# First mixer of a two-layer encoder: score matmuls of two heads interleaved, division moved behind the values, state reordering split over two engines, ten low weight parts written by an accumulating DMA

## The chip, the cores and the metric

The kernel runs as one program on one core of one Trainium2 chip. The metric is the device time of one execution in microseconds, the median of three runs. TensorE (PE) does the matmuls, ScalarE (ACT) and VectorE (DVE) the elementwise work, GpSimd (POOL) some more of it, and SyncE (SP) issues nearly all DMAs.

## The reference, cut to what matters

Two layers over 512 positions of width 1024. The change lies in the first mixer alone: an 8-head neighbourhood attention beside a bidirectional S5 state recurrence, both fed by one input projection.

```python
def na_s5_mixer(h, w_in, ...):
    z = h @ w_in                                   # 1024 -> 4 x 512
    q, k, v, u = jnp.split(z, 4, axis=-1)
    a_out = neighbourhood_attention(q, k, v, rpb)  # 8 heads of 64
    b_out = s5_glu(s5_bidirectional(u, ...), w_glu, b_glu)
    return jnp.concatenate([a_out, b_out], -1) @ w_out

# attention, per head and row of the 8 x 64 grid
logits = q_row . k_window * dh**-0.5 + bias        # 8 x 16 window
probs  = softmax(logits)
out    = probs @ v_window

# S5, per direction, 32 groups of 16 channels, 64 states
bu     = b_bar @ u
states = associative_scan(lam_bar, bu)
y     += real(c @ states)
```

After the mixer come, per layer, a gated MLP and a per-layer embedding p that is projected to the model width; the second layer has a retention mixer. The change touches none of them.

## The kernel before, in words

All matrix products of the projections are done in split precision: weights and activations are kept as a high part and a low part, and `mm3` (L134 to L137) issues three matmuls for each product, low weight by high activation (L135), high by high (L136) and high weight by low activation (L137), all into one PSUM bank.

The weights lie in DRAM as 241 chunks of 128x1024 (512 KB, eight 128x128 tiles each) in the order of use. For each chunk SP issues the load into a raw buffer `wr` (L98, three buffers), ACT copies the high part `wh` (L113), and DVE subtracts the low part `wl` = `wr` - `wh` (L115 for chunks 1 to 3, L117 after that). `wh` and `wl` have four buffers each, so chunk c can be split once PE has finished chunk c-4; `weights()` asks for the split three chunks ahead. Chunks 0 to 3 give U (the input of the recurrence), 4 to 11 give q and k, 12 to 15 give v, 16 to 19 the projections of p, 20 to 23 the first half of the output projection.

The first mixer, in the order of its code:

- U projection, then `u_out` (DVE, L162 inside a helper): U times the normalising row, written to DRAM and read back in another layout (SP). It needs the row `rr`, which ACT copies at L249.
- q and k, eight outputs n = 0 to 7 (DVE L679 or L162 reads each out of PSUM). Between them DVE builds the weights of the recurrence: `prep_w1` (four products, two sums), which `trans_w1` transposes on PE (L481) and ACT copies (L483); with them `states` (PE, L585) makes the inputs of the recurrence into `XV`. `prep_w2` (three DVE operations of 128x512) makes the output weights; the table `W2_K` says how many after each n.
- v, four banks at once, and among it the `local` steps of the recurrence (four DVE operations each).
- Thirteen score steps. Step h of 0 to 7 does `scores(h)`: eight matmuls for one head (L752; 64 of the 128 rows hold the head, rows 0 to 63 for an even head, 64 to 127 for an odd one), a DVE reduction with the bias (L758) and an ACT exponential (L761, which also gives the sums). `scale(h)` (DVE) takes reciprocals of the sums and multiplies the exponentials. `transp(h-3)` transposes them on PE (L778) and ACT copies the result (L780). `values(m)` for two heads (L797) multiplies with v, and ACT (high) and DVE (low) split the result straight out of PSUM. Between these lie `strips` (PE L501, ACT L504 into the table `Tm`), the carry steps of the recurrence (`carry`, four DVE operations of 128x512 each, seven in all, placed by `CARRY_A` and `CARRY_F`), and `fill(n)`: n outputs of the projection of p, six matmuls each, which are independent work for PE. When all eight strips are done, `toeplitz` sends `Tm` through DRAM and back (SP, eight loads, L526).
- `first_half(n)`, the first half of the output projection, six of them; after the fifth `phases(b)` reorders the finished states `XV` into matmul operands, on ACT (L884 for partitions 0 to 63, L886 for 64 to 127, eight each).
- `y_mm` (PE, L904, 96 matmuls in 192 records), which needs U, `Tm`, the w2 weights and the reordered states, and gives the output of the recurrence.

The code states this order, but a scheduler decides on each engine what stands next (up to the end of `u_out` the order of ACT and DVE is as written). PSUM has eight banks of 128x512, the pool of 128x512 tiles in SBUF 53.

Of the kernel before, what the change touches and what calls it, by code (L numbers as in the profile page):

```python
# [41 lines left out]
SPLIT_AHEAD = 3  # L42
GLU_AT = 10
FILL = (0,) + (1,) * 11
W2_K = (0, 0, 0, 1, 1, 2, 2, 2)
W2_A = (1, 1, 1, 1, 1, 1, 1, 1, 0, 0, 0, 0, 0)
CARRY_A = (0, 0, 0, 0, 0, 0, 0, 0, 1, 1, 1, 1, 1)
LOCAL_V = (1, 2, 2, 2)
CARRY_F = (1, 1, 0, 0, 0)
HELD = 5  # L50
LAG = 3
HOLD = 2
# [3 lines left out]
DO_W = 6  # L56
PLE_POOL = 3
NOLAG = 7


@with_exitstack
def trunk_kernel(ctx, tc, xn, xp, pT, wts, vec, s5bc, ddiag, bias, cs, dst, ident, out):
# [20 lines left out]
    def PS():  # L83
        seq[0] += 1
        return pp.tile([128, 512], F32, name=f"ps{seq[0]}", tag="ps")
# [22 lines left out]
    def w_split1(c):  # L108
        w_dma(c)
        raw = raws.pop(c)  # L110
        h = wspl.tile([128, 1024], F32R, name=f"wh{c}", tag="wh")
        l = wspl.tile([128, 1024], F32R, name=f"wl{c}", tag="wl")
        act.activation(out=h, in_=raw, func=ACTF.Copy)  # L113
        if c < 4:
            dve.tensor_tensor(out=l, in0=raw, in1=f(h), op=ALU.subtract)  # L115
        else:
            late.append(lambda: dve.tensor_tensor(out=l, in0=raw, in1=f(h), op=ALU.subtract))  # L117
            if len(late) > 1:
                late.pop(0)()
        parts[c] = (h, l)  # L120
        st["split"] += 1
        w_dma(c + RAW_BUFS)
# [38 lines left out]
    def tt(eng, out, a, b, op):  # L161
        eng.tensor_tensor(out=out, in0=a, in1=b, op=op)  # L162
# [117 lines left out]
    def mixer0():  # L280
# [455 lines left out]
        P2 = {}  # L736
        PTs = {}

        def scores(h):
            rows = slice(64 * (h % 2), 64 * (h % 2) + 64)  # L740
            q, k = qt[h // 2], kt[h // 2]
            bt = bts.pop(h)
            bias_load(h + 2)
            for half in range(2):
                ps = PS()
                for i in range(2):
                    b = 2 * half + i
                    if b < 3:
                        lhs, rhs = q[rows, 64 + 128 * b:192 + 128 * b], k[rows, 128 * b:128 * b + 256]
                    else:  # L750
                        lhs, rhs = qe[h // 2][rows], k[rows].rearrange("p (a t) -> p a t", t=128)[:, ::3, :]
                    pe.matmul(out=ps[:, 256 * i:256 * i + 256], lhsT=lhs, rhs=rhs, start=True, stop=True)  # L752
                P = T()
                for i in range(2):
                    b = 2 * half + i
                    v = 256 * (b == 3)

                    dve.tensor_tensor_reduce(out=P[:, 256 * i:256 * i + 256], in0=ps[:, 256 * i:256 * i + 256],  # L758
                                             in1=bt[:, v:v + 256], scale=-1.0, scalar=3e38, op0=ALU.add,
                                             op1=ALU.min, accum_out=mx[:, h, b:b + 1])  # L760
                    act.activation(out=P[:, 256 * i:256 * i + 256], in_=P[:, 256 * i:256 * i + 256], func=ACTF.Exp,  # L761
                                   scale=-1.0, bias=mx[:, h, b:b + 1], accum_out=sums[:, h, b:b + 1])
                P2[h, half] = P

        def scale(h):
            for half in range(2):
                P = P2[h, half]
                dve.reciprocal(out=sums[:, h, 2 * half:2 * half + 2], in_=sums[:, h, 2 * half:2 * half + 2])
                sc = sums[:, h, 2 * half:2 * half + 2].rearrange("p (a o) -> p a o", o=1).to_broadcast([128, 2, 256])
                Pv = P.rearrange("p (a k) -> p a k", a=2)  # L770
                tt(dve, Pv, Pv, sc, ALU.mult)

        def transp(h):
            for half in range(2):
# [7 lines left out]

        def values(m):

            ps = PS()
# [14 lines left out]
            for e in range(2):  # L800
                for half in range(2):
                    PTs.pop((2 * m + e, half))
            h_, l_ = T(F32R), T(F32R)
            act.activation(out=h_, in_=ps, func=ACTF.Copy)
            tt(dve, l_, ps, f(h_), ALU.subtract)
            mix.append((h_, l_))

        kept = []

# [26 lines left out]

        for step in range(10 + LAG):
            if step < 8:
                scores(step)
            if LAG <= step < 8 + LAG:  # L840
                transp(step - LAG)
            next_w2(W2_A[step])
            if step == 2:
                fk_load(1)
            if step == 6:
                prep_chunk()
            if step < 8:
                scale(step)
            run("carry", CARRY_A[step])
            if step >= LAG + 2 and (step - LAG) % 2 == 0:  # L850
                values((step - LAG) // 2 - 1)
            next_strips()
            if step < len(FILL):
                fill(FILL[step])
            if step >= 9:
                x_load(2)
        fill(16)
        keep()
        fk.clear()
# [10 lines left out]
                    between(k)  # L870
            tt(dve, xr[n], ps, xr[n], ALU.add)


        sph = {}

        def phases(b):
            gs = slice(8 * b, 8 * b + 8)
            for c in range(2):
                t = T()
                v = t.rearrange("p (g c) -> p g c", c=64)  # L880
                eng = dve
                eng.memset(v[0:64, :, 0:1], 0.0)
                eng.memset(v[64:128, :, 63:64], 0.0)
                act.activation(out=v[0:64, :, 1:64], in_=XV[0:64, c, 0:63, gs].rearrange("p c g -> p g c"),  # L884
                               func=ACTF.Copy)
                act.activation(out=v[64:128, :, 0:63], in_=XV[64:128, c, 62::-1, gs].rearrange("p c g -> p g c"),  # L886
                               func=ACTF.Copy)
                sph[b, c] = v

        flat = XV.rearrange("p a b c -> p (a b c)")  # L890
        G = flat[:, 0:2048].rearrange("p (m j i n) -> p m j i n", m=2, j=8, n=16)
# [31 lines left out]
                        dve.tensor_copy(YG[:, 2 * m + e, 4 * jh:4 * jh + 4, :], src)  # L923

        for n in range(HELD):
            run("carry", CARRY_F[n])
            first_half(n)
        for b in range(4):
            phases(b)
        first_half(HELD)  # L930
        for m in range(2):
            for i in range(8):
# [438 lines left out]
```

## Time and profile before

| what | value |
|---|---|
| median of 3 runs | 1541.13 us (1540.98 to 1542.32) |
| the profiled execution | 1541.97 us, span 1540.2 us |
| PE busy | 1501.5 us, 97% of the span |
| DVE, ACT, POOL busy | 928.9, 613.6, 355.1 us |
| mean granted TensorE clock | 0.988 of full speed |

A trace row gives a start, a duration, the engine, the line of the kernel, and output and inputs by the program's names. "Idle before" is the time in which the engine stood still ahead of an instruction, with what ended it. The granted clock is that of TensorE as a share of full speed (2.4 GHz); 0.5 is its lower level (1.2 GHz).

### The profile page before, as it was taken

The page shows a single profiled execution, that of the slowest core. Times are in us where ns is not written, and L with a number is a line of the kernel's source. Part 1 is how long each engine was busy: PE and PEld are TensorE (multiplying, and loading weights), DVE is VectorE, ACT ScalarE, POOL GpSimd, SP SyncE. Part 2 cuts the span into 40 slices and gives each one's busy share as a digit, 9 for nine tenths or more (in the row PEclk, how much of TensorE's full clock was granted, in tenths as well). Part 3 has the DMA queues.
Part 4 walks back from the last instruction along what each step waited for, and adds up shares of the span by engine and source line. Part 5 has one row for each costly group of instructions (what it writes and reads, how often), then busy time and mean ns, then how long its engine had stood idle before and what let it go on. Part 6 is the DMA issues. An engine that isn't in the chain of part 4 may idle for free.

```text
span 1540.2 us, 18035 instructions
## 1 busy us (share of the span) xinstructions
PE 1501.5 (97%) x7088; PEld 1237.5 (80%) x7088; DVE 928.9 (60%) x1247; ACT 613.6 (40%) x853; POOL 355.1 (23%) x246
## 2 busy tenths in 40 slices
PE   7899989999999999999999999999999999999997
PEld 5787767888888888887888888888888888888886
DVE  8888974786776633476454454535367767643336
ACT  5244647454444422343425242423244444432233
POOL 0000000233232311054123141504223232312105
PEclk9899999999999999999999999999999999999999
DMA  5514191333333433433222222222333333333341
GB/s 194 150 56 154 62 249 44 96 96 98 98 102 98 119 97 96 129 107 106 83 69 82 69 82 69 83 69 82 96 96 96 96 97 97 98 96 92 99 133 55
DMA packets 57493, 153.69 MB, mean 100 GB/s; under 512 B 11584, under 2 KB 15808, under 8 KB 57408
## 3 DMA queue, kind: packets, MB, share of 16 engines
q1 hardware_dynamic: 57408, 152.55, 32.8%
q8 instruction: 55, 0.90, 0.3%
q14 instruction: 30, 0.25, 0.1%
HBM read 144.69 MB, written 7.83 MB: 99 GB/s over the span
## 4 chain that ended last, share of the span: by engine, by line
PE 81%; issue 7%; DVE 6%; DMA 2%; ACT 2%; POOL 1%; SPq 1%; DVEq 0%; POOLq 0%
PE ps L135 26%; PE ps L137 26%; PE ps L136 26%; DVE t L162 3%; PE ps L585 1%; DVE wl L117 1%; DMA wr<-in_wts_dram 1%; DMA Tm<-k_scr 1%; PE ps L752 1%; DVE t L271 1%; ACT t L884 0%; ACT t L886 0%; PE ps L778 0%; PE ps L235 0%; PE ps L481 0%
## 5 line engine op out<-in xcount | busy, mean ns | idle before, releaser
L135 PE MATMUL ps<-t,wl 128*128 128x512 f32 x1568 | 615.9, 393 | 9.6 <-DVE wl L545 7.0
L136 PE MATMUL ps<-t,wh 128*128 128x512 f32 x1568 | 611.5, 390 | 0.0
L137 PE MATMUL ps<-t,wh 128*128 128x512 f32 x1568 | 608.8, 390 | 0.7 <-DVE t L271 0.7
L117 DVE TENSOR_TENSOR wl<-wr,wh 128x1024 fp32r<-128x1024 f32 x238 | 310.2, 1305 | 306.6 <-ACT wh L113 306.4
L113 ACT ACTIVATE wh<-wr 128x1024 fp32r<-128x1024 f32 x241 | 254.6, 1059 | 583.9 <-PE ps L137 281.9
L135 PEld LDWEIGHTS ps<-t,wl 128*128 128x128 f32 x1568 | 296.1, 189 | 73.2 <-DVE wl L545 7.0
L137 PEld LDWEIGHTS ps<-t,wh 128*128 128x128 f32 x1568 | 296.0, 189 | 63.6 <-DVE t L271 1.8
L136 PEld LDWEIGHTS ps<-t,wh 128*128 128x128 f32 x1568 | 296.3, 189 | 60.3
L162 POOL TENSOR_TENSOR t<-t,t 128x512 f32<-128x512 f32 x117 | 178.1, 1524 | 457.7 <-ACT t L995 279.5
L162 DVE TENSOR_TENSOR t<-ps,t 128x512 f32<-128x512 f32 (+2 forms) x86 | 59.3, 699 | 108.5 <-PE ps L137 100.0
L162 DVE TENSOR_TENSOR t<-t,t 128x512 f32<-128x512 f32 (+2 forms) x113 | 96.9, 877 | 27.8 <-ACT t L194 20.7
L162 DVE TENSOR_TENSOR pad<-ps,t 128x512 f32<-128x512 f32 x88 | 60.6, 692 | 82.7 <-PE ps L137 82.7
L991 DVE SCALAR_TENSOR_TENSOR t<-pad,vecs,t 128x512 f32<-128x512 f32 x88 | 102.2, 1164 | 1.5
L162 POOL TENSOR_TENSOR t<-t 128x512 f32<-128x512 f32 x33 | 50.4, 1529 | 189.9 <-DVE t L162 189.9
L135 PE MATMUL ps<-e,wl 128*128 128x512 f32 x216 | 85.4, 395 | 0.0
L137 PE MATMUL ps<-e,wh 128*128 128x512 f32 x216 | 85.3, 395 | 0.0
L136 PE MATMUL ps<-e,wh 128*128 128x512 f32 x216 | 85.2, 395 | 0.0
L169 POOL TENSOR_TENSOR t<-t,t 128x512 fp32r<-128x512 f32 x41 | 58.5, 1444 | 60.4 <-ACT t L168 51.7
L992 DVE SCALAR_TENSOR_TENSOR t<-pad,vecs,t 128x512 f32<-128x512 f32 x88 | 70.0, 796 | 2.9
L989 ACT ACTIVATE t<-pad,vecs 128x512 f32<-128x512 f32 x88 | 70.2, 802 | 3.4 <-DVE pad L162 3.4
L162 POOL TENSOR_TENSOR r<-v,mhalf 128x4 f32<-128x4 f32 x10 | 17.8, 1777 | 206.0 <-DVE v L239 206.0
L135 PE MATMUL ps<-wh,t 128*128 128x512 f32 x160 | 62.6, 391 | 0.0
(209 smaller groups left out, 1365.2 us busy)
## 6 DMA issues: line engine op xcount, KB each, us to landing
wr<-in_wts_dram SPq DMA_DIRECT2D x241, 512.0 KB, 3.7
pj_scr<-t SPq DMA_DIRECT2D x16, 256.0 KB, 4.8
t<-pj_scr SPq DMA_DIRECT2D x16, 256.0 KB, 4.5
t<-in_xp_dram SPq DMA_DIRECT2D x8, 256.0 KB, 5.4
t<-in_bias_dram SPq DMA_DIRECT2D x8, 256.0 KB, 3.9
Tm<-k_scr SPq DMA_DIRECT2D x8, 256.0 KB, 7.6
t<-in_xn_dram SPq DMA_DIRECT2D x8, 256.0 KB, 7.3
out_dram<-t SPq DMA_DIRECT2D x8, 256.0 KB, 2.4
```

What stands on the lines that cost most here:

```text
L113: act.activation(out=h, in_=raw, func=ACTF.Copy)
L117: late.append(lambda: dve.tensor_tensor(out=l, in0=raw, in1=f(h), op=ALU.subtract))
L135: pe.matmul(out=ps, lhsT=lhs[1], rhs=rhs[0], start=start, stop=False)
L136: pe.matmul(out=ps, lhsT=lhs[0], rhs=rhs[0], start=False, stop=False)
L137: pe.matmul(out=ps, lhsT=lhs[0], rhs=rhs[1], start=False, stop=stop)
L162: eng.tensor_tensor(out=out, in0=a, in1=b, op=op)
L169: low.tensor_tensor(out=l, in0=src, in1=f(h), op=ALU.subtract)
L271: self.late.append(lambda: dve.scalar_tensor_tensor(out=l, in0=x, scalar=g, in1=f(h), op0=ALU.mult, op1=ALU.subtract))
L585: pe.matmul(out=pw[:, i, :], lhsT=w1t["ri"[c], g // 4][:, 128 * (g % 4):128 * (g % 4) + 128], rhs=U[:, g, :], start=True, stop=True)
L989: act.activation(out=c, in_=t[:, 1:513], func=ACTF.Identity, scale=vcol(cw + 44 + j), bias=vcol(V_CB + 44 * i + j))
L991: dve.scalar_tensor_tensor(out=c, in0=t[:, 0:512], scalar=vcol(cw + j), in1=c, op0=ALU.mult, op1=ALU.add)
L992: dve.scalar_tensor_tensor(out=c, in0=t[:, 2:514], scalar=vcol(cw + 88 + j), in1=c, op0=ALU.mult, op1=ALU.add)
```

## The change

1. **Low parts of chunks 6 to 15.** ACT writes `wl` = -`wr` (rounded as the high part is), and a DMA on POOL's queue adds the weights from DRAM into it. Ten DVE subtractions go; ten ACT operations of 128x1024 and ten accumulating transfers of 512 KB come.
2. **Scores.** `scores(m)` issues the sixteen matmuls of two heads together, alternately on rows 0 to 63 and 64 to 127, into four PSUM banks; the softmax part is `soft(h)`.
3. **Division.** `scale` goes (sixteen DVE products of 128x512). `values(m)` spreads the reciprocal sums over a second bank `pr` with eight matmuls (L801 of the changed kernel), ACT copies it, DVE multiplies it with the values, and the product is split. Per pair of heads that is one ACT copy and one DVE product more, and one bank.
4. **Tables.** Three `prep_w2` move from the score steps into the q and k part; all seven carries run in steps 5 to 11; `prep_chunk` (small DVE operations that the carries need) moves from step 6 to step 3.
5. **Phases.** They move ahead of `fill(16)`, each with one fill behind it, and the half for partitions 64 to 127 is copied by DVE.

```diff
-W2_K = (0, 0, 0, 1, 1, 2, 2, 2)
-W2_A = (1, 1, 1, 1, 1, 1, 1, 1, 0, 0, 0, 0, 0)
-CARRY_A = (0, 0, 0, 0, 0, 0, 0, 0, 1, 1, 1, 1, 1)
+W2_K = (0, 0, 0, 1, 1, 3, 3, 3)
+W2_A = (1, 1, 1, 1, 1, 0, 0, 0, 0, 0, 0, 0, 0)
+CARRY_A = (0, 0, 0, 0, 0, 1, 1, 1, 1, 1, 1, 1, 0)
-CARRY_F = (1, 1, 0, 0, 0)
+WL_DMA = (6, 16)
...
         act.activation(out=h, in_=raw, func=ACTF.Copy)
-        if c < 4:
+        if WL_DMA[0] <= c < WL_DMA[1]:
+            while late:
+                late.pop(0)()
+
+            act.activation(out=l, in_=raw, func=ACTF.Copy, scale=-1.0)
+            pool.dma_start(out=l, in_=wts[c], accum_op=ALU.add)
+        elif c < 4:
             dve.tensor_tensor(out=l, in0=raw, in1=f(h), op=ALU.subtract)
...
+        def scores(m):
+            for half in range(2):
+                for e in range(2):
+                    sps[2 * m + e, half] = PS()
+                for i in range(2):
+                    b = 2 * half + i
+                    for e in range(2):
+                        rows = slice(64 * e, 64 * e + 64)
...
+                        pe.matmul(out=sps[2 * m + e, half][:, 256 * i:256 * i + 256], lhsT=lhs, rhs=rhs,
+                                  start=True, stop=True)
...
-        def scale(h):
-            for half in range(2):
-                P = P2[h, half]
-                dve.reciprocal(out=sums[:, h, 2 * half:2 * half + 2], in_=sums[:, h, 2 * half:2 * half + 2])
-                sc = sums[:, h, 2 * half:2 * half + 2].rearrange("p (a o) -> p a o", o=1).to_broadcast([128, 2, 256])
-                Pv = P.rearrange("p (a k) -> p a k", a=2)
-                tt(dve, Pv, Pv, sc, ALU.mult)
...
-            ps = PS()
+            ps, pr = PS(), PS()
+            for b in range(4):
+                for e in range(2):
...
+                    pe.matmul(out=o, lhsT=sums[:, 2 * m + e, b:b + 1].to_broadcast([128, 64]), rhs=idn,
+                              start=True, stop=True)
+            rs = T()
+            act.activation(out=rs, in_=pr, func=ACTF.Copy)
...
-            h_, l_ = T(F32R), T(F32R)
-            act.activation(out=h_, in_=ps, func=ACTF.Copy)
-            tt(dve, l_, ps, f(h_), ALU.subtract)
-            mix.append((h_, l_))
+            tt(dve, rs, ps, rs, ALU.mult)
+            mix.append(split(rs))
...
             if step < 8:
-                scores(step)
+                if step % 2 == 0:
+                    scores(step // 2)
+                soft(step)
...
-            if step == 6:
+            if step == 3:
                 prep_chunk()
             if step < 8:
-                scale(step)
+                dve.reciprocal(out=sums[:, step, :], in_=sums[:, step, :])
...
-                act.activation(out=v[64:128, :, 0:63], in_=XV[64:128, c, 62::-1, gs].rearrange("p c g -> p g c"),
-                               func=ACTF.Copy)
+                dve.tensor_copy(v[64:128, :, 0:63], XV[64:128, c, 62::-1, gs].rearrange("p c g -> p g c"))
...
+        for b in range(4):
+            phases(b)
+            fill(1)
+        fill(16)
...
         for n in range(HELD):
-            run("carry", CARRY_F[n])
             first_half(n)
-        for b in range(4):
-            phases(b)
         first_half(HELD)
```

Lines behind the first hunks stand some 6 lower in the changed kernel, later ones up to 22 (L752 of before is L761, L904 is L926). Where the change moves instructions, the built order shows it at three places.

DVE from the end of U's normalisation (`r50` is the row's source; `ps38` to `ps49` are the four U banks that `u_out` reads), before:

```order
L117 TENSOR_TENSOR wl6_395<-wr6_258,wh6_394 128x1024
L117 TENSOR_TENSOR wl7_439<-wr7_326,wh7_438 128x1024
L117 TENSOR_TENSOR wl8_517<-wr8_362,wh8_516 128x1024
L162 TENSOR_TENSOR t54_475<-ps38_287,t53_473 128x512
L162 TENSOR_TENSOR t55_479<-ps43_322,t53_473 128x512
L162 TENSOR_TENSOR t56_483<-ps46_357,t53_473 128x512
L162 TENSOR_TENSOR t57_487<-ps49_393,t53_473 128x512
```

Three subtractions of 128x1024 stand ahead of the four rows of `u_out`; the same place in the changed kernel, and further on the first weights of the recurrence (`t58` and `t60` are what PE transposes first):

```order
L168 TENSOR_TENSOR t54_478<-ps38_287,t53_476 128x512
L168 TENSOR_TENSOR t55_482<-ps43_322,t53_476 128x512
L168 TENSOR_TENSOR t56_486<-ps46_357,t53_476 128x512
L168 TENSOR_TENSOR t57_490<-ps49_393,t53_476 128x512
...
L685 SCALAR_TENSOR_TENSOR t68_550<-ps67_518,t53_476 128x512
L168 TENSOR_TENSOR t58_496<-t58_496,t59_497 128x512
L168 TENSOR_TENSOR t73_566<-p1r_131,t39_312 128x512
L168 TENSOR_TENSOR t74_567<-p1i_132,t41_317 128x512
L168 TENSOR_TENSOR t75_571<-p1r_131,t41_317 128x512
L168 TENSOR_TENSOR t76_572<-p1i_132,t39_312 128x512
L168 TENSOR_TENSOR t60_501<-t60_501,t61_502 128x512
```

The subtractions are gone, wl9 (which stood just ahead of the sum t58) too, and t58, which came behind all twelve products, now comes ahead of the last four.

ACT at the same place (`t53` is the row `rr` that `u_out` waits for, L255 of the changed kernel, L249 of before), in the changed kernel:

```order
L113 ACTIVATE wh6_394<-wr6_258 128x1024
L118 ACTIVATE wl6_395<-wr6_258 128x1024
L113 ACTIVATE wh7_440<-wr7_326 128x1024
L118 ACTIVATE wl7_441<-wr7_326 128x1024
L118 ACTIVATE wl8_520<-wr8_362 128x1024
L113 ACTIVATE wh8_519<-wr8_362 128x1024
L255 ACTIVATE t53_476<-ps52_471 128x512
L118 ACTIVATE wl9_598<-wr9_400 128x1024
```

Before, only wh6, wh7 and wh8 stood ahead of the row; now an operation of 128x1024 more stands behind each raw load, and chunk 8 has two ahead of the row.

PE at the start of the score steps (`t106` is k of heads 0 and 1, `t62` their q), before:

```order
L752 MATMUL ps194_1281<-t106_764,t62_503 128x256 x2
L752 MATMUL ps196_1289<-t106_764,t62_503 128x256
L752 MATMUL ps196_1289<-t106_764,qe0_1265 128x256
L501 MATMUL ps200_1306<-t99_718,t77_576 32x128 x4
L501 MATMUL ps200_1306<-t113_802,t79_584 32x128 x4
L752 MATMUL ps202_1318<-t106_764,t62_503 128x256 x2
L752 MATMUL ps204_1326<-t106_764,t62_503 128x256
L752 MATMUL ps204_1326<-t106_764,qe0_1265 128x256
```

Each head stands in one block with strips between them. The same place in the changed kernel:

```order
L761 MATMUL ps199_1304<-t106_771,t62_506 128x256
L761 MATMUL ps200_1305<-t106_771,t62_506 128x256
L761 MATMUL ps199_1304<-t106_771,t62_506 128x256
L761 MATMUL ps200_1305<-t106_771,t62_506 128x256
L761 MATMUL ps201_1310<-t106_771,t62_506 128x256
L761 MATMUL ps202_1311<-t106_771,t62_506 128x256
L761 MATMUL ps201_1310<-t106_771,qe0_1290 128x256
L761 MATMUL ps202_1311<-t106_771,qe0_1290 128x256
```

The two heads now alternate from row to row, and the strips have moved behind them; the second pair of heads alternates only in part (two rows of one head, two of the other).

ACT at the phases, before (L823 copies a fill's bank, L113 splits a chunk):

```order
L823 ACTIVATE t356_2045<-ps355_2038 128x512
L113 ACTIVATE wh24_2096<-wr24_1892 128x1024
L113 ACTIVATE wh25_2130<-wr25_2007 128x1024
L884 ACTIVATE t366_2149<-XV_84 64x8x63
L886 ACTIVATE t366_2149<-XV_84 64x8x63
L884 ACTIVATE t367_2154<-XV_84 64x8x63
L886 ACTIVATE t367_2154<-XV_84 64x8x63
```

All sixteen stand in one block behind the last fill and behind chunk 25. The same work in the changed kernel (L887 is the half that ACT keeps, L840 copies a fill's bank):

```order
L804 ACTIVATE t350_1997<-ps349_1988 128x512
L174 ACTIVATE t351_2016<-t350_1997 128x512
L840 ACTIVATE t354_2027<-ps353_2020 128x512
L887 ACTIVATE t359_2038<-XV_84 64x8x63
L887 ACTIVATE t360_2043<-XV_84 64x8x63
L840 ACTIVATE t362_2055<-ps361_2048 128x512
L887 ACTIVATE t363_2058<-XV_84 64x8x63
L887 ACTIVATE t364_2063<-XV_84 64x8x63
L840 ACTIVATE t366_2081<-ps365_2068 128x512
L887 ACTIVATE t367_2084<-XV_84 64x8x63
L113 ACTIVATE wh23_2136<-wr23_1670 128x1024
```

The eight that ACT keeps have moved up among the last fills' copies, five of them ahead of chunk 23 and none behind chunk 24.

## Rows read from the trace of the kernel before

**Rows 1.** Head of the page: busy us, share of the span, instructions.

```profile
PE 1501.5 (97%) x7088; PEld 1237.5 (80%) x7088; DVE 928.9 (60%) x1247; ACT 613.6 (40%) x853; POOL 355.1 (23%) x246
```

**Rows 2.** Stretches: length, engines' busy us (instructions), granted clock, DMA share, GB/s.

```profile
60.00:80.00 20.00, 18.02 (x79) 16.23 (x80) 14.83 (x28) 6.13 (x13) 0.00 (x0) 0.66 0.16 53
...
140.00:160.00 20.00, 16.09 (x119) 11.20 (x118) 19.48 (x63) 15.17 (x46) 0.00 (x0) 0.89 0.43 145
...
220.00:240.00 20.00, 12.64 (x120) 10.73 (x118) 5.42 (x23) 14.81 (x15) 0.00 (x0) 0.74 0.39 153
```

**Rows 3.** PE's waits from 0 to 280 us: total, times, longest.

```profile
PE ps L481 <- DVE t L162: 5.4, 1, 5.4
...
PE ps L778 <- DVE t L162: 3.9, 2, 2.5
...
PE ps L904 <- ACT t L886: 8.8, 4, 3.2
```

**Rows 4.** The chain that ended last, 38 to 76 us: start, duration, what.

```profile
47.47 3.97 DVE t L162 x4
...
60.19 1.14 DVE wl L117
...
61.98 1.97 PE ps L481 x8
63.95 3.31 PE ps L585 x16
...
74.75 0.23 PE ps L137
```

**Rows 5.** ACT in order of time, 30 to 46 us.

```profile
31.48 2.96 ACT L113 ACTIVATE wh<-wr 128x1024 fp32r<-128x1024 f32 x3
...
44.57 1.06 ACT L113 ACTIVATE wh<-wr 128x1024 fp32r<-128x1024 f32 x1 [1.98 <-DMA wr<-in_wts_dram]
45.54 0.58 ACT L249 ACTIVATE t<-ps 128x512 f32<-128x512 f32 x1
```

**Rows 6.** Stretches of 2 us, columns as in the second group.

```profile
70.00:72.00 2.00, 2.00 (x10) 1.90 (x10) 2.00 (x4) 1.48 (x3) 0.00 (x0) 0.50 0.85 217
...
156.00:158.00 2.00, 1.23 (x8) 0.90 (x12) 2.00 (x8) 1.70 (x8) 0.00 (x0) 0.50 0.00 0
...
162.00:164.00 2.00, 2.00 (x9) 1.43 (x8) 1.75 (x6) 0.64 (x2) 0.00 (x0) 0.88 0.50 140
```

**Rows 7.** PE in order of time, at 139, 169 and 188 us.

```profile
139.55 1.56 PE L752 MATMUL ps<-t,t 64*128 64x256 f32 x6
140.95 0.59 PE L752 MATMUL ps<-t,qe 64*128 64x256 f32 x2
...
169.10 1.09 PE L778 MATMUL ps<-idn,t 128*128 128x128 f32 x8
170.12 1.97 PE L797 MATMUL ps<-t,t 128*64 128x128 f32 x32
...
188.80 0.43 PE L501 MATMUL ps<-t,t 128*32 128x128 f32 x8
```

**Rows 8.** Groups by line and shape, 139 to 171 us: busy, mean ns.

```profile
L758 DVE CUSTOM_DVE_ANT_0 t<-ps,t 128x256 f32<-128x256 f32 x24 | 9.0, 418 | 0.6 <-PE ps L752 0.5
```

**Rows 9.** The chain that ended last, 200 to 250 us.

```profile
202.69 8.98 DMA Tm<-k_scr
...
225.08 1.07 ACT t L884
...
242.32 4.58 PE ps L904 x78
```

**Rows 10.** The line L904: its matmuls with `Tm`, duration, first and last start.

```profile
L904 PE MATMUL ps<-Tm,U x64: 272/273/475, 223.0 to 246.2; 128*64 128x128 f32 x64
```

**Rows 11.** DMA issues of the page: count, KB each, us to landing.

```profile
wr<-in_wts_dram SPq DMA_DIRECT2D x241, 512.0 KB, 3.7
...
Tm<-k_scr SPq DMA_DIRECT2D x8, 256.0 KB, 7.6
```

More of the change, by code (lines that the diff above doesn't have):

```diff
@@ L737, in mixer0, with soft @@
         PTs = {}
-        def scores(h):
-            rows = slice(64 * (h % 2), 64 * (h % 2) + 64)
-            q, k = qt[h // 2], kt[h // 2]
+        sps = {}
+        def scores(m):
[6 more added lines that the diff above has]
+                        rows = slice(64 * e, 64 * e + 64)
+                        q, k = qt[m], kt[m]
+                        if b < 3:
+                            lhs, rhs = q[rows, 64 + 128 * b:192 + 128 * b], k[rows, 128 * b:128 * b + 256]
+                        else:
+                            lhs, rhs = qe[m][rows], k[rows].rearrange("p (a t) -> p a t", t=128)[:, ::3, :]
+                        pe.matmul(out=sps[2 * m + e, half][:, 256 * i:256 * i + 256], lhsT=lhs, rhs=rhs,
+                                  start=True, stop=True)
+        def soft(h):
             bt = bts.pop(h)
@@ L744, in scores @@
             for half in range(2):
-                ps = PS()
[L746 to L752, printed above, removed]
+                ps = sps.pop((h, half))
                 P = T()
@@ L783, in values @@
         def values(m):
-            ps = PS()
+            ps, pr = PS(), PS()
+            for b in range(4):
+                for e in range(2):
+                    ov = pr[64 * e:64 * e + 64, :].rearrange("p (r c) -> p c r", c=64)
+                    if b < 3:
+                        o = ov[:, 8 + 16 * b:24 + 16 * b, :]
+                    else:
+                        o = ov.rearrange("p (a e) r -> p a e r", e=8)[:, ::7]
+                    pe.matmul(out=o, lhsT=sums[:, 2 * m + e, b:b + 1].to_broadcast([128, 64]), rhs=idn,
+                              start=True, stop=True)
+            rs = T()
+            act.activation(out=rs, in_=pr, func=ACTF.Copy)
             for half in range(2):
@@ L856, in mixer0, with phases @@
                 x_load(2)
+        sph = {}
+        def phases(b):
+            gs = slice(8 * b, 8 * b + 8)
+            for c in range(2):
+                t = T()
+                v = t.rearrange("p (g c) -> p g c", c=64)
+                eng = dve
+                eng.memset(v[0:64, :, 0:1], 0.0)
+                eng.memset(v[64:128, :, 63:64], 0.0)
+                act.activation(out=v[0:64, :, 1:64], in_=XV[0:64, c, 0:63, gs].rearrange("p c g -> p g c"),
+                               func=ACTF.Copy)
+                dve.tensor_copy(v[64:128, :, 0:63], XV[64:128, c, 62::-1, gs].rearrange("p c g -> p g c"))
+                sph[b, c] = v
+        for b in range(4):
+            phases(b)
+            fill(1)
         fill(16)
@@ L871, in first_half @@
             tt(dve, xr[n], ps, xr[n], ALU.add)
[L874 to L884, printed above, removed]
-                               func=ACTF.Copy)
-                act.activation(out=v[64:128, :, 0:63], in_=XV[64:128, c, 62::-1, gs].rearrange("p c g -> p g c"),
-                               func=ACTF.Copy)
-                sph[b, c] = v
         flat = XV.rearrange("p a b c -> p (a b c)")
```

## Prediction

> **What bounds the kernel now.** I read the page's busy times first, then PE's busy time and clock by stretches, then PE's waits, then the chain of work in the stretches where PE stood still. The reader should see that PE is the limit: it is busy 1501.5 us, 97% [rows 1]. So little can be won outside PE's gaps. They lie in the first mixer, and each has a second cost behind it, the clock.
>
> - Gap A, at 57 us: PE waits 5.4 us for a DVE result that its first transposes need [rows 3]. The chain shows why: `u_out` at 47.47, behind it the products for the first weights, one more subtraction (wl9, 1.14), and only then the transposes at 61.98 and the states at 63.95 [rows 4]. The clock is still 0.50 in 70 to 72 us [rows 6], and averages 0.66 over 60 to 80 [rows 2].
> - Gap B, 140 to 162 us: PE waits 3.9 us in two pieces for DVE before it can transpose the first exponentials [rows 3]. DVE is busy 19.48 of the 20 us from 140 on [rows 2]: `scale` stands in its queue behind other work. The clock falls to 0.50 in 156 to 158 us and is still 0.88 on average in 162 to 164 [rows 6].
> - Gap C, 223 to 247 us: the first matmuls of `y_mm` start at 223.0, the last with `Tm` at 246.2 [rows 10], while ACT copies the phases one by one from 225.08, 1.07 us each [rows 9]; 8.8 us of PE's waits there name L886 outright [rows 3], and the clock averages 0.74 [rows 2].
>
> Behind 260 us the program is untouched, and I count nothing there.
>
> **The change part by part.**
>
> *A: low parts by DMA.* Ten DVE subtractions of 1.14 us go. Ahead of the states four of them stood on DVE: wl6 to wl8 before `u_out`, wl9 after it. The first three win nothing, because `u_out` also waits for the row that ACT copies at 45.54 [rows 5], and ACT now has an operation more ahead of it. Chunk 8's raw load lets ACT begin at 44.57 [rows 5]; two operations of 1.06 and the row's 0.58 end at 47.3, against a start of `u_out` at 47.47 [rows 4]. So DVE starts at the same time. Between `u_out`'s end at 51.44 and wl9 at 60.19 lie fifteen operations in 8.75 us, 0.58 each [rows 4]. The first sum now stands ahead of the last four products and without wl9, so the first transposes can start 1.14 + 4 x 0.58 = 3.5 us earlier; the second sum, for the transposes that the states need, stands behind them all and wins 1.14 plus a copy between the two sums that now comes later (0.28 to 0.58). I take 1.6 us. The low end is a loss of 2 (ACT, with twice the work per chunk, late with the row by one more operation of 1.06, and the read-back of U late by one more load on SP's queue), the high end is this and the clock: at 0.50, the work from 61.98 to 72 takes 10 us for 5 at full speed, so 1.6 + 5 = 6.6.
>
> What the ten transfers cost: ACT's ten further operations lie beside PE and ACT was idle 13.87 of 20 us in 60 to 80 [rows 2]. If that cover were gone, 10 x 1.06 = 10.6 us. Each transfer must land before its chunk is used. No accumulating transfer and none on POOL's queue stands in the trace; the nearest rows are the raw loads (512 KB in 3.7 us) and `Tm` back from DRAM (256 KB in 7.6) [rows 11]. By these I bound one transfer between 3.7 and 15.2 us (twice the second, for twice the bytes). A chunk's buffers come free three chunks ahead, 72 matmuls of 0.23 us at full clock [rows 4], 5.5 us a chunk or 16.6 in all. Within these bounds less the 2.1 us of ACT none is late as long as they don't queue up behind one another: term 0, the rest under the rivals. On POOL's queue the root that the row needs stands behind the first transfer, four clears of tiles behind the next three: an issue that holds POOL delays the row and so `u_out` by as much, which the low end of -2 covers.
>
> Of this the Trainium skill speaks in "SBUF — State Buffer", section "SBUF: two separate sides": a transfer issued from POOL's queue has its descriptors written by POOL, which is locked out while DVE runs a two-port operation, so that one of 620 ns took 3100 ns beside a DVE copy. By that rule the transfers would stretch wherever DVE runs copies; the trace has no transfer of this kind with which to agree or not. By the same skill's "DMA: Bandwidth & Descriptors", section on the anatomy of one such DMA, 512 KB would take about 2.0 + 1.2 = 3.2 us, an estimate from its fit, and the term would stay 0.
>
> *B: scores, division, tables.* The first transposes no longer wait for `scale` in a full DVE queue, and three `prep_w2` leave that queue as well. I take the 3.9 us back, and the half clock that followed: in 156 to 158 PE ran 1.23 us, in 162 to 164 a mean of 0.88 is 0.5 us at half [rows 6], with the 4 us between some 5.7 us at half speed, so 2.8 lost. Interleaved scores: one head takes 2.0 us of PE (139.55 to 140.95 + 0.59, six records and two [rows 7]), eight heads 16. If rows 0 to 63 and 64 to 127 work side by side, half of it goes, 8; if not, nothing. No row has two row halves together. The nearest pair is `values`, whose matmuls alternate between the two halves of the output columns and take 1.97/32 = 62 ns a record, against 1.09/8 = 136 ns for whole transposes of the same 128 columns [rows 7]: side by side, they run at under half. I take 6 of 8, since one pair of heads in four does not alternate throughout. What the division adds on PE: eight matmuls per pair of heads, of the same form as those of `values`, 16 records of 62 ns, 1.0 us, four times 4.0.
>
> The Trainium skill bears on the first of these: "TensorE: Matmul & The Clock Gate", "Part 3: Packing small matmuls — row/col tiling", says that matmuls on different row groups of the array run at the same time, four of them measured 3.07 times as fast. The row of column halves points the same way, and by two full halves the term would be 8, not 6.
>
> New waits: a pair of heads now holds four PSUM banks at once until DVE has reduced them, at 0.42 us each quarter [rows 8]; eight quarters are 3.4 us, and PE has two strips and one fill to do between. The next `values` wants two banks. I take 3 us for these, between 0 and 6. B is then 3.9 + 2.8 + 6 - 4.0 - 3 = 5.7 us, with ends of 3.9 + 2.8 + 0 - 4.0 - 6 = -3.3 and 3.9 + 2.8 + 8 - 4.0 = 10.7.
>
> *C: phases ahead.* `y_mm` takes 23.9 us from its first start at 223.0 [rows 10] to its end at 246.9. Its last 78 records took 4.58 us [rows 9], so all 192 need 11.3: 12.6 us to win. For that its inputs must be there when PE comes, at about 223.0 - 1.6 - 5.7 = 215.7. The last carry stands beside values(3) in DVE's new order; from there PE has three fills and six `first_half`, 18 + 72 matmuls or 20.7 us. ACT's eight phases of 1.07 [rows 9] with four bank copies between them need about 11, DVE's eight run beside them (no row for that copy; DVE's other strided copies are shorter than ACT's 1.07, and at 1.07 each it is 8.6). The margin is some 9 us. `Tm`: its last strips now stand ten fills, two `values`, six `first_half` and 24 transposes ahead of `y_mm`, some 39 us (132 x 0.23, 2 x 3.0 and 24 x 0.136); before, they stood at 188.80 [rows 7] and `Tm` landed at 202.69 + 8.98 = 211.7 [rows 9], 22.9 later. So both inputs are early and I take all 12.6; half of it if one is late.
>
> *Sum.* 1.6 + 5.7 + 12.6 = 19.9 us. The profiled execution's own time of 1541.97 (its span and 1.77 around it) less this is 1522.1; the median of the runs shown is 0.84 lower, so I predict 1521 (1521.2).
>
> **The rivals.**
>
> 1. *The transfers queue up (slower).* If POOL's queue moves them one after the other at L us each, the first starts when ACT has written wl6, at 31.48 + 2.96 + 1.06 = 35.5 [rows 5], and the tenth lands at 35.5 + 10 L. Chunk 15 is needed a chunk ahead of the first score, at 139.55 - 5.5 = 134.0 [rows 7]. Nothing is lost up to L = 9.9; at L = 11.9 the 20 us are gone; at the bound of 15.2 the tenth lands at 187.5, 53 late, and the time is 1521 + 53 = 1574. For it: a read, an addition and a write, in a queue for which there is no row. The rule of the Trainium skill's "SBUF — State Buffer" above would be a way to it. Against: 512 KB in 3.7 us, and DMA engines 16% busy in that stretch [rows 2]. 6%.
> 2. *Row halves don't overlap.* The term of 6 falls away: 1527. For it: no row shows it. Against: the column halves. 14%.
> 3. *Gap A heals with its clock.* The transposes that come 3.5 us earlier split the wait, and if the clock stays up another 5 us come: 1516. 10%.
> 4. *`y_mm` still waits.* DVE, which keeps the carries and now takes half the phases, or SP's queue is late with one input: 6 of 12.6 us, 1527. For it: DVE's load [rows 2]. Against: the margins. 9%.
> 5. *Nothing is won, the stall only moves:* the PSUM banks and DVE hold the score steps so long that B is -3.3 and phases are late as well: 1521 + 9 + 6 = 1536 or more. 4%.
>
> **How the numbers follow.** The forecast itself has 57%, with a range of its own of 1516 to 1526. The 80% range takes in rivals 2 to 4 with their own spread: 1511 to 1531. This kernel's runs spread 0.1%, and I call 0.2% (3 us) the least that can be told from no change. Slower by more than that needs rival 1 beyond L = 12.2: 5%. Within it: the rest of rivals 1 and 5, 2%. Faster: 93%.
>
> **What would show it.** In the changed kernel's trace: first states (L591) at about 62 us; no wait of L786 on DVE's products near 152; a pair of heads' scores in about 2.4 us, not 4; `y_mm` (L926) in one run of about 11 us from about 215, at clock 1.00; PE's wait on a low part of chunks 6 to 15 none; the transfers landing in under 10 us each. The prediction is wrong if L141 waits for a transfer between 50 and 139 us, if the scores take 2 us per head as before, or if L926 begins on time and then stops for L887, L889 or `Tm`.

## The result and the profile after

The changed kernel takes 1528.34 us (median of four runs, 1527.03 to 1530.21), the kernel before in the same comparison 1541.72: the ratio is 0.9913, 95% interval 0.9894 to 0.9932. That is 13.4 us won, where 20 were forecast. The profiled execution shown here took 1527.03 us.

The head of its page and two of its DMA rows (count, KB, median us to landing):

```profile
span 1525.2 us, 18170 instructions
...
PE 1495.3 (98%) x7152; PEld 1234.6 (81%) x7152; DVE 915.7 (60%) x1225; ACT 615.1 (40%) x859; POOL 363.9 (24%) x256
...
wl<-in_wts_dram POOLq DMA_DIRECT2D x10, 512.0 KB, 7.5
...
Tm<-k_scr SPq DMA_DIRECT2D x8, 256.0 KB, 6.7
```

PE is still the limit. Its busy time is 6 us lower than in [rows 1]; the rest of the gain is idle time that is gone. The same stretches as in [rows 2], with 160 to 180 us added:

```profile
60.00:80.00 20.00, 16.03 (x63) 13.88 (x64) 13.82 (x28) 6.14 (x12) 0.86 (x1) 0.58 0.68 169
140.00:160.00 20.00, 19.15 (x176) 14.23 (x174) 19.57 (x58) 15.96 (x47) 0.00 (x0) 1.00 0.58 187
160.00:180.00 20.00, 17.05 (x202) 13.41 (x198) 19.70 (x73) 15.85 (x46) 0.00 (x0) 1.00 0.23 78
220.00:240.00 20.00, 20.00 (x242) 18.18 (x241) 7.75 (x13) 9.85 (x16) 0.00 (x0) 1.00 0.15 48
```

Gap C is gone: PE is busy throughout 220 to 240 us at full clock. Gap B keeps its clock, though PE is still idle 0.85 + 2.95 us beside a DVE that is as full as before. Gap A has become worse: less PE work, a clock of 0.58 instead of 0.66, and the DMA engines 68% busy instead of 16%. PE's waits from 0 to 100 and 100 to 200 us, which answer to [rows 3]:

```profile
PE ps L487 <- DVE t L168: 6.2, 2, 4.3
...
PE ps L786 <- ACT t L804: 1.4, 1, 1.4
```

The chain that ended last from 46 to 74 us, against [rows 4] and [rows 5]:

```profile
46.01 0.59 ACT wl L118
...
46.96 1.04 ACT wh L113
48.00 0.49 ACT t L255
...
48.51 4.06 DVE t L168 x4
52.57 2.72 DVE t L331
55.29 2.40 DVE t L168 x4
...
64.95 1.12 PE ps L487 x4
...
66.20 7.06 PE ps L591 x32
```

ACT's row is there at 48.5, `u_out` starts 1.0 us later than before, and the small operation behind it (L331), which takes 0.42 us in e1 and e8 below, takes 2.72 on the chain (2.80 by its own record). POOL in order of time says what ran beside it:

```profile
52.22 0.85 POOL L119 DMA_DIRECT2D wl<-in_wts_dram  x1 [3.96 <-ACT wl L118]
52.75 2.25 POOL L443 MEMSET t<- 128x512 f32 x4
```

The four clears had moved behind wl9's transfer, and so beside L331. The states start at 66.20 instead of 63.95, 32 records at half clock, and the first score comes at 142.95 instead of 139.55 [rows 7]. The scores themselves, and the line of `y_mm` (duration, first and last start):

```profile
142.95 1.57 PE L761 MATMUL ps<-t,t 64*128 64x256 f32 x12
144.34 0.60 PE L761 MATMUL ps<-t,qe 64*128 64x256 f32 x4
144.87 1.08 PE L507 MATMUL ps<-t,t 128*32 128x128 f32 x32
```

```profile
L926 PE MATMUL ps<-Tm,U x64: 272/273/323, 220.6 to 230.5; 128*64 128x128 f32 x64
```

Two heads take 1.92 us (142.95 to 144.87), the time of one before. `y_mm` runs from 220.6 to some 231.3 (its last matmul starts at 231.0), 10.7 us, where it took 23.9.

The balance by stages of the two profiled executions: up to the first score 139.55 to 142.95, 3.4 us lost; from there to `y_mm` 83.5 to 77.7, 5.8 won; `y_mm` 23.9 to 10.7, 13.2 won. That makes 15.6 where the spans differ by 15.0. The 0.6 is lost behind `y_mm`, in the untouched rest of the program, which takes between 1293.3 and 1295.0 us in the fourteen profiled executions of this document.

### The profile page after: what moved, and what is told of

Same layout as the page of the kernel before. It is cut to its first block, busy times and chain, and to the rows that moved or that the text cites. A ratio compares the mean times of both kernels' runs of the same rounds, so it can differ in the third digit from the quotient of the medians.

```text
span 1525.2 us, 18170 instructions
## 1 busy us (share of the span) xinstructions
PE 1495.3 (98%) x7152; PEld 1234.6 (81%) x7152; DVE 915.7 (60%) x1225; ACT 615.1 (40%) x859; POOL 363.9 (24%) x256
## 3 DMA queue, kind: packets, MB, share of 16 engines
q1 hardware_dynamic: 57408, 152.55, 32.9%
q0 software_dynamic: 1440, 5.24, 2.1%
## 4 chain that ended last, share of the span: by engine, by line
PE 84%; DVE 7%; issue 6%; DMA 1%; POOL 1%; ACT 1%; SPq 0%; DVEq 0%; POOLq 0%; ACTq 0%
PE ps L141 27%; PE ps L143 27%; PE ps L142 27%; DVE t L168 4%; PE ps L591 1%; PE ps L926 1%; DMA t<-in_xp_dram 1%; DVE wl L123 1%; DVE t L277 1%; DVE t L774 0%; PE ps L816 0%; PE ps L241 0%; PE ps L487 0%; POOL t L175 0%; DMA vecs<-in_vec_dram 0%
## 5 line engine op out<-in xcount | busy, mean ns | idle before, releaser
L113 ACT ACTIVATE wh<-wr 128x1024 fp32r<-128x1024 f32 x241 | 254.4, 1059 | 556.2 <-PE ps L143 277.5
L123 DVE TENSOR_TENSOR wl<-wr,wh 128x1024 fp32r<-128x1024 f32 x228 | 298.2, 1309 | 288.9 <-ACT wh L113 288.8
L168 DVE TENSOR_TENSOR t<-ps,t 128x512 f32<-128x512 f32 (+1 forms) x86 | 59.3, 698 | 114.8 <-PE ps L143 103.4
L143 PE MATMUL ps<-wl,t 128*128 128x512 f32 x160 | 62.3, 389 | 0.0
```

The source lines that it names most:

```text
L143: pe.matmul(out=ps, lhsT=lhs[0], rhs=rhs[1], start=False, stop=stop)
```

## The experiments

All ratios are to the kernel before, measured beside it; the changed kernel stands at 0.9913. Where `first score`, `states` or `y_mm` times are given, they are of the run's profiled execution.

| run | median us | ratio (95%) | first score | y_mm from |
|---|---|---|---|---|
| changed kernel | 1528.34 | 0.9913 (0.9894 to 0.9932) | 142.95 | 220.6 |
| e1 all low parts on DVE | 1524.43 | 0.9884 (0.9868 to 0.9899) | 140.0 | 218.1 |
| e2 transfers from chunk 10 | 1524.36 | 0.9880 (0.9863 to 0.9896) | 140.6 | 218.2 |
| e3 kernel before, transfers alone | 1546.21 | 1.0021 (1.0007 to 1.0036) | 140.0 | 223.2 |
| e4 phases late, all on ACT | 1528.11 | 0.9902 (0.9887 to 0.9917) | 144.9 | 222.5 |
| e5 heads one after the other | 1527.24 | 0.9904 (0.9887 to 0.9920) | 144.3 | 221.9 |
| e6 division on the exponentials | 1532.18 | 0.9937 (0.9923 to 0.9952) | 143.0 | 226.5 |
| e7 carries as before | 1528.06 | 0.9917 (0.9897 to 0.9937) | 141.0 | 215.7 |
| e8 L331 ahead of u_out | 1528.17 | 0.9915 (0.9900 to 0.9930) | 143.5 | 221.1 |
| e9 carries and phases as before | 1536.42 | 0.9967 (0.9957 to 0.9977) | 140.5 | 215.2 |
| e10 e1, transposes one output later | 1516.89 | 0.9841 (0.9826 to 0.9855) | 129.2 | 210.0 |
| e11 e2, transposes one output later | 1512.99 | 0.9815 (0.9800 to 0.9829) | 127.6 | 206.8 |
| e12 e11, carries as before | 1515.10 | 0.9814 (0.9799 to 0.9829) | 128.7 | 203.4 |

**Gap A: what do the transfers cost?**

```diff
-WL_DMA = (6, 16)
+WL_DMA = (6, 6)
```

> The changed kernel with all low parts subtracted by DVE again (no accumulating transfers, no negated copies on ACT); all else as changed. Theory T (the ten transfers cost more at gap A than DVE's relief wins: the first score came at 142.95 us instead of 139.55): without them the row for u_out is at about 45.5 again, the scaling of the output weights (L331) takes 0.4 us and not 2.8, U is written and read back without other transfers beside it, and the first score is back near 139.5; 1528.3 - 3.4 = 1525, between 1523 and 1527. Rival R (DVE needs the relief, since three prep_w2 more now lie in the q and k part: 12 us of subtractions come back): states and scores wait for DVE, 1531 to 1535.

1524.43 us, 3.9 less than the changed kernel; the states start at 63.5 and the first score comes at 140.0. Theory T holds; R doesn't, though the twelve microseconds of subtractions are back on DVE.

```diff
-WL_DMA = (6, 16)
+WL_DMA = (10, 16)
```

> The changed kernel with the transfers for chunks 10 to 15 only; chunks 6 to 9 are subtracted by DVE. Theory T: gap A is that of the kernel before (first transposes at 62 us, first score at about 139.5), and DVE still has six subtractions (7 us) less before the scores: 1523 to 1526. Rival (the transfers harm wherever they run, or the loss at gap A has another cause, such as the order of the sums): 1528 or more, first score at 142 or later.

1524.36 us, first score 140.6. The transfers of chunks 10 to 15 cost nothing and, against e1, win nothing. So it is the first four that harm.

The kernel before with L118 and L119 of the change and nothing else:

```diff
-        if c < 4:
+        if WL_DMA[0] <= c < WL_DMA[1]:
...
+            act.activation(out=l, in_=raw, func=ACTF.Copy, scale=-1.0)
+            pool.dma_start(out=l, in_=wts[c], accum_op=ALU.add)
+        elif c < 4:
```

> The kernel before with the ten transfers for chunks 6 to 15 and nothing else of the change. Theory T: the first score comes 2 to 4 us later than in the kernel before, at 142 to 143.5, and the time is 1543 to 1546; DVE's relief of 12 us wins nothing by itself. Rival (the transfers pay, as I predicted with 1.6 us, and the loss at gap A comes from the tables that are not in this kernel): 1538 to 1541.

Slower by a ratio of 1.0021, with its interval clear of 1. Its ten runs lie between 1540.69 and 1550.30, a spread that no other run here has. T is right in the sign of the time, but not in the place: the profiled execution, near the quick end, has its first score at 140.0, where 142 to 143.5 was expected, and its `y_mm` ends at 246.6, no later than before (246.9). Where the slower ones lose their time is not shown.

What the transfers cost does change from execution to execution. The changed kernel, e4, e5, e6, e7 and e9 have the same instructions in the same order up to the first score, and yet it comes at 142.95, 144.9, 144.3, 143.0, 141.0 and 140.5. Against 139.55 before, gap A loses between 0.9 and 5.4 us; the 3.4 of the profile above is one value out of this range.

What is it that they delay? In the changed kernel two things are late together. On DVE's chain (the row, L331 beside POOL's clears) the second transposes end at 66.07; on U's way through DRAM its first part is read back from 61.9 and lands 4.2 us later, at 66.1. The states start behind both, at 66.20, so this profile alone can't tell them apart. e8 takes the collision of L331 away:

```diff
+        ts(cim, cim, -1.0)
         for m in range(4):
             u_out(m)
-        ts(cim, cim, -1.0)
```

> The changed kernel with the negation of one of the output weights' factors (L331) ahead of u_out, where DVE waits for the row anyway; behind u_out it took 2.80 us beside POOL's clears instead of 0.42. Theory M2 (this collision is what makes gap A longer): the chain on DVE is 2.8 us shorter, the first score comes near 140, 1525 to 1526. Theory M1 (the transfers slow the way of U through DRAM, 11.6 us to landing instead of 4.6, and U is there only at 66 us or later): the states start at 66 us or later still, the first score stays at 142 to 145, 1527 to 1530.

1528.17 us, no change. PE in order of time in e8:

```profile
57.74 0.65 PE L487 MATMUL ps<-idn,t 128*128 128x128 f32 x4 [2.69 <-DVE t L168]
60.74 1.12 PE L487 MATMUL ps<-idn,t 128*128 128x128 f32 x4 [2.35 <-DVE t L168]
67.21 3.01 PE L591 MATMUL ps<-U,t 128*128 128x64 f32 x13 [5.35 <-DMA U<-u_scr]
```

Here the first transposes start at 57.74, near the 58.5 that the prediction worked out (61.98 - 3.5), and then PE stands 5.35 us more for U. The chain that ended last in e8 leads from U's write through its read-back to the states:

```profile
48.08 12.25 DMA u_scr<-t
...
60.35 6.72 DMA U<-u_scr
...
67.21 7.06 PE ps L591 x32
```

The same wait is named in e4 (5.4 us), e5 (3.2) and e6 (5.3); in e4 and e6 L331 had begun early enough to take 0.41 and 0.43 us, and the states were late all the same. The write of U to DRAM, its landing times in the changed kernel and then in e1 (minimum, median, maximum):

```profile
L566 SPq DMA_DIRECT2D u_scr<-t x4: 320/323/331, 49.6 to 52.6; - x4
...
DMA to landing us min/median/max: 11.0/11.6/12.3
```

```profile
L566 SPq DMA_DIRECT2D u_scr<-t x4: 319/322/331, 48.2 to 51.2; - x4
...
DMA to landing us min/median/max: 3.9/4.3/4.9
```

U's write takes 11.6 us instead of 4.3, its read-back is issued at 61.9 instead of 53.1, and the states wait. What holds it up is seen in the DMA queues from 50 to 56 us (packets, MB, share of the 16 DMA engines' time), in the kernel before and then in the changed one; q1 carries what SP issues, q0 what POOL issues:

```profile
q1 hardware_dynamic: 1747, 1.91, 92.4%
```

```profile
q0 software_dynamic: 231, 0.88, 79.2%
q1 hardware_dynamic: 95, 0.39, 17.6%
```

The engines had no room there before the change either. Now the accumulating transfers take 79.2% of them for 0.88 MB, and 0.39 MB of everything else gets through instead of 1.91. Over the whole program they take nearly twice as long per MB as the rest (2.1% of the span for 5.24 MB, 32.9% for 152.55). So M1 is shown.

**The score steps: which part wins the 5.8 us?**

```diff
-            for half in range(2):
-                for e in range(2):
-                    sps[2 * m + e, half] = PS()
...
+            for e in range(2):
+                for half in range(2):
+                    for i in range(2):
```

> The changed kernel with the sixteen score matmuls of a pair in the order head by head instead of alternating on the row halves; the same four banks. Theory S (the row halves work side by side: the changed kernel's pairs took 1.92, 1.92, 2.7 and 1.92 us, 8.5 in all, where eight single heads take 15.4): 6.9 us more PE work, of which the waits of 3.8 us between 140 and 180 us can hide some: 1531 to 1535, and a pair takes 3.8 us. Rival (the score steps go at DVE's pace, which is busy 19.6 of 20 us there, so that PE's time does not count): 1527 to 1530.

1527.24 us, no difference that these runs can tell: the rival holds. First score to `y_mm` is 77.6 us, as in the changed kernel. A pair took 2.9 us here (144.29 to 147.19), not 3.8, since the second head overlaps the first at the seam. What PE works more, it waits less (columns as in [rows 2]):

```profile
140.00:160.00 20.00, 20.00 (x155) 15.51 (x154) 19.57 (x57) 15.55 (x44) 0.00 (x0) 1.00 0.51 171
160.00:180.00 20.00, 18.75 (x196) 14.79 (x197) 19.70 (x71) 15.86 (x47) 0.00 (x0) 1.00 0.29 93
```

PE's idle time falls from 3.8 to 1.25 us, DVE's busy time is the same to the digit: DVE sets this stage.

```diff
+        def scale(h):
...
+                tt(dve, Pv, Pv, sc, ALU.mult)
...
-            ps, pr = PS(), PS()
+            ps = PS()
...
-                dve.reciprocal(out=sums[:, step, :], in_=sums[:, step, :])
+                scale(step)
```

> The changed kernel with the division back where it was: DVE multiplies the exponentials (sixteen products), no sums spread by PE, values split straight from PSUM. Theory D (DVE sets the score steps): sixteen products of 0.6 us more and four fewer, 7 us of DVE in a stretch where it has no room, and the transposes wait for them again: 1533 to 1538. Rival (PE sets them; the 64 records for the sums cost it 4 us): 1524 to 1527.

1532.18 us, 3.8 more than the changed kernel and a little under theory D's range (1533 to 1538), and the stage takes 83.5 us, as long as before the change. PE's waits from 140 to 215 us:

```profile
PE ps L794 <- DVE sums L784: 5.5, 1, 5.5
PE ps L507 <- DVE t L168: 4.7, 1, 4.7
```

Theory D: without the sixteen DVE products the stage is 5.8 us shorter, and the 4 us of PE that the division costs in their place are covered. That this is also the gain of the whole stage is a coincidence of two other terms, as e7 shows below.

**`y_mm`: carries or phases?**

```diff
+        for b in range(4):
+            phases(b)
         first_half(HELD)
...
-                dve.tensor_copy(v[64:128, :, 0:63], ...)
+                act.activation(out=v[64:128, :, 0:63], ...)
```

> The changed kernel with the phases at their old place in the code (behind the fifth first_half) and all sixteen copies on ACT; carries early as changed. Theory C1 (y_mm's gap closed because the carries end at 201 us instead of 225): the sixteen copies of 1.07 us, 17.1 in all, can start as soon as ACT is done with the fills, near 208, and end near 225; the second half of y_mm needs the last of them at 226: at most 3 us lost, 1528 to 1532. Rival C2 (the move of the phases ahead of the fills and the split over two engines is what pays): y_mm takes 20 us or more again, 1536 to 1541.

1528.11 us; `y_mm` runs from 222.5 to 233.2 without a stop. C1 holds.

```diff
-CARRY_A = (0, 0, 0, 0, 0, 1, 1, 1, 1, 1, 1, 1, 0)
+CARRY_A = (0, 0, 0, 0, 0, 0, 0, 0, 1, 1, 1, 1, 1)
+CARRY_F = (1, 1, 0, 0, 0)
...
+            run("carry", CARRY_F[n])
             first_half(n)
```

> The changed kernel with the carries (and the small operations that they need) at their old steps, two of them in the first halves, and so the phases behind the fifth first half, still split over ACT and DVE. Theory C1 (y_mm's gap closed because the carries end early): the last carry ends near 222 us, eight copies of 1.07 us on ACT follow, y_mm starts near 222 and ends near 236 to 240 instead of 231, its clock falls: 1533 to 1538. Rival C3 (two engines for the phases are enough): 1528 to 1530.

1528.06 us: C1 falls, as far as it made the early carries the one cause. The stage before is 3 us shorter with the carries at their old steps (74.7 us), so the early carries cost 3 us there. If the parts add up, the changed kernel wins another 3 us in that stage beside the division's 5.8; interleaving is not it (e5), the three moved `prep_w2` may be, and no run tries them alone. `y_mm` starts at 215.7 and ends near 229.6, with these waits only:

```profile
PE ps L924 <- ACT t L888: 1.8, 2, 1.3
PE ps L924 <- DVE t L890: 0.5, 1, 0.5
```

Both undone together:

> The changed kernel with both undone that e4 and e7 undid one at a time: carries at their old steps, phases behind the fifth first half and all on ACT. Either alone cost nothing that the runs can tell (1528.1 and 1528.1). Theory C4 (each of the two alone closes y_mm's gap): y_mm stops for ACT's sixteen copies again, about 20 us long instead of 10.5 to 13.6, at a fallen clock: 1534 to 1540. Rival (the gap closed because score steps and DVE are lighter, and neither matters): 1527 to 1530.

1536.42 us, C4 holds. `y_mm` is some 25 us long again (215.2 to 240.4), with the wait of [rows 3] back:

```profile
PE ps L925 <- ACT t L890: 9.5, 4, 3.8
```

Gap A differs from one execution to the next, so the time from the first score to the end of `y_mm` says more than the medians: 88.3 us in the changed kernel and in e4, 88.6 in e7, 99.9 in e9.

**A better order for gap A.** PE asks for the first weights of the recurrence right behind the second q output. e10 and e11 ask one output later:

```diff
-            if n:
-                after_trans(n - 1)
+            if n > 1:
+                after_trans(n - 2)
             next_w2(W2_K[n])
+        after_trans(6)
         after_trans(7)
```

> All low parts on DVE as in e1, and the transposes and states of the recurrence one output of q and k later, so that PE has 24 matmuls (5.5 us) to do at 57 us where it stood still. Theory G (gap A is only an order: PE asks for the first sums one output too early): no wait of the transposes, no fall of the clock at 60 to 73 us, the first score some 8 to 10 us earlier unless DVE (89 of 100 us busy from 40 to 140) becomes the bound: 1515 to 1520. Rival (DVE sets the q and k part, the wait only moves): 1523 to 1526.

1516.89 us; the first score comes 10.8 us ahead of e1's, and 7.5 of them are left in the time.

> As e10, but with the transfers for chunks 10 to 15, which take 7 us off DVE. Theory G with DVE as the next bound: 1 to 4 us better than e10, 1513 to 1518. Rival (DVE is no bound there, or the transfers delay a chunk now that PE is earlier): no better than e10.

1512.99 us. The stretch from 60 to 80 us of e11:

```profile
60.00:80.00 20.00, 20.00 (x125) 17.64 (x123) 19.82 (x37) 11.56 (x19) 3.63 (x4) 1.00 0.77 185
```

PE is busy throughout at full clock; DVE has become nearly as full as PE (19.82 of 20 us), and now the six late transfers, worth nothing in e2, are worth 3.9 us. Theory G holds in both.

> e11 with the carries at their old steps and the phases behind the fifth first half, split over ACT and DVE (as e7). Theory D (DVE sets the pace of the score steps, 19.7 of 20 us busy): without most of the carries there, the stretch from the first score to y_mm is some 3 us shorter, as in e7 (74.7 us against 77.6), and y_mm gives 2 to 3 us of it back by its own waits: 1510 to 1513. Rival (PE sets it by now, and the late carries cost y_mm more): 1514 to 1517.

1515.10 us, which lies in the rival's range (1514 to 1517), but the ratio is that of e11 (0.9814 and 0.9815), since the kernel before was slower on that chip as well. The stretch to `y_mm` was 74.7 us as theory D had it, and `y_mm` gave it back (from 203.4 to 218.6, 15.3 us). Inconclusive between the two: no difference that these runs can tell.

## Why the prediction was right or wrong

The time lies in the range (1511 to 1531), faster as forecast, outside the likeliest case's own 1516 to 1526; two thirds of the forecast gain came.

- **Term A, +1.6 forecast, -3.4 in the profile (-0.9 to -5.4 over six executions): the step that failed.** The step is "none is late as long as they don't queue up behind one another: term 0". It asked only whether a transfer lands before its own chunk is used. They do: 7.5 us, at most 11.1, no wait of PE on them. But the same DMA engines carry U to DRAM and back at that very moment, and U's write went from 4.3 to 11.6 us (e1 and the changed kernel), which e8 shows to be enough by itself to hold the states. I had read the free DMA share from 60 to 80 us (16%); the transfers of chunks 6 to 9 start at 36 to 52, and from 50 to 56 the engines were 92% busy already before the change. The low end of -2 did count U's read-back as late, but by one load only; it was issued 8.3 us later than before (61.9 against 53.6).
- The row for `u_out` was 1.0 us late in this execution, not on time: ACT's row of 47.3 became 48.5. In e3 to e9 the write that follows it is first issued at 47.8 to 49.0, against 48.5 before, so this is no steady loss. The clears behind wl9's transfer hit L331. Taking that collision away won nothing (e8), since U was late as well.
- **Term B, +5.7 forecast, +5.8 in the profile: right in sum by luck, wrong in its parts.** The 6 us for interleaved scores are saved on PE (6.8: the pairs took 1.9, 2.0, 2.7 and 1.9 us, 8.6 against eight times 1.92) and are worth nothing in time (e5), because DVE is 98% busy from 140 to 180 us. The new waits for PSUM banks came to 0.8 us, not 3. The division's DVE products are worth 5.8 (e6; 3.8 in the medians), the early carries cost 3.0 (e7), which the term did not count, and by difference some 3 us more are won, which no run here separates; what the moved `prep_w2` add was not tried alone.
- **Term C, +12.6 forecast, +13.2 in the profile: right.** ACT's last phase ended at 212.5, 8.1 us ahead of PE, where 9 were worked out. What I missed is that it was won twice over: early carries (e4) or split phases (e7) each do it alone, and both undone cost 8.1 us in the medians and 11.6 from the first score to the end of `y_mm` (e9).
- Rival 1's mechanism (a queue on POOL) came in small: the transfers of chunks 7, 8 and 9, issued at 46.4, 47.4 and 52.2, landed one after the other at 54.6, 58.5 and 61.7. They landed 3 to 4 us apart, far below the 9.9 from which the rival counted a loss, so its price was not paid. By the Trainium skill's "DMA: Bandwidth & Descriptors", section on the anatomy of one such DMA, a transfer was estimated at 3.2 us; the trace has 7.5. The lock between DVE and POOL in the Trainium skill's "SBUF — State Buffer", section "SBUF: two separate sides", agrees with what L331 shows, the other way round from the case that the prediction cited: DVE's operation took 2.80 us beside POOL's clears and ended 0.28 us after the last of them, and took 0.42 in e8, where no clear ran beside it. On the transfers no run here shows it apart from the shared DMA engines.
- Rival 2 is refuted: the halves overlap fully (1.92 us for two heads), but its price of 6 us was wrong as well. Rival 3 did not come: the transposes' wait was split in two, the clock fell all the same (0.58). Nor did rival 4 (`y_mm` ran without a stop) or rival 5.

Open: why e3 scatters over 10 us. That the way of U varies from run to run would fit (PE's wait for it is 0.8 us in e7 and 5.4 in e4, with the same instructions up to there), but only the profiled executions show it, and e3's own lost nothing up to the end of `y_mm`.

## What to carry to other kernels

Here a transfer that took work off an engine was paid for by what else was on the DMA engines in the same microseconds: look up the DMA round trips on the path at that time, not only when the transfer's own result is needed. Before pricing a saving on PE, find what the engine beside it does in that stretch: at 98% DVE, 6.8 us of PE were worth nothing and sixteen products on DVE were worth 5.8. And try the order first where an order makes the gap: asking one output later won 7.5 us (e1 to e10), while making the late sums 4.2 us earlier won nothing (e8).

## What the runs showed of the hardware

- An accumulating 512 KB transfer from POOL's queue landed in 7.5 us (5.3 to 11.1) against 3.6 for a plain load of the same size, over the whole program, and these transfers kept the DMA engines busy nearly twice as long per MB as the rest.
- Beside them, a 256 KB write from SBUF to DRAM landed in 11.6 us, and in 4.3 without them (e1).
- Matmuls on 64 rows each, alternating between the two row halves: the 16 records of two heads took 1.92 us together, the time of the 8 records of one head alone. Head by head they took 2.9 (e5).
- A DVE operation of 0.42 us took 2.80 beside four POOL clears, and 1.67 in e5.
- DVE's reordering copy of 64x504 took 0.62 us, ACT's 1.13 beside it and 1.06 alone (in the kernel before).
